# Two binary searches in an encoder step: VectorE's six tiles in one group, ScalarE on one tile throughout, and another order of masks and attention

## Chip, core and metric

The kernel runs on one core of a Trainium2 chip. The metric is the device time of one execution in microseconds. Engines go by the profile's names: PE is TensorE (PEld its weight loads), DVE is VectorE, ACT is ScalarE, POOL is GpSimd, and SP is SyncE, whose queue issues the transfers.

## What is computed

One layer of a streaming encoder on 1,024 prompt frames and 64 sample frames: a half-step feed-forward block, an input projection, a sparse attention branch and a convolution branch merged by gates, a second half-step block and a final normalization. The part that the change touches is the choice of keys:

```python
limit = (pos // CHUNK + 1) * CHUNK
admissible = key_pos[None, :] < limit[:, None]
s = jnp.einsum('bqhd,bsd->bqhs', qi, k_idx).astype(jnp.float32)
score = jnp.einsum('bqh,bqhs->bqs', wi.astype(jnp.float32), jax.nn.relu(s))
score = jnp.where(admissible[None], score, -jnp.inf)
_, sel = lax.top_k(score, top)             # top = min(256, L // 4)
...
p = jax.nn.softmax(logits, axis=-1)        # over the selected keys alone
o = jnp.einsum('bqcgn,bqncd->bqcgd', p, vg)
```

## The kernel before

**Search tiles.** `STILES` has seven tiles of query rows with their scores: tiles 0 to 5 have 128 rows and 384, 512, 640, 768, 896 and 1,024 keys; tile 6 is the sample, 64 rows and 192 keys. (The first 256 prompt rows need no search.) Attention numbers the same rows by `ATILES`: search tile n is attention tile n + 2, so that the widest is attention tile 7 and the sample is attention tile 8.

**The search.** The kernel finds, for each row, the value of its top-th score, bit by bit: first the 15 upper bits (`search(15, ...)`), then, after `low_half` has counted the rows above and taken out the lower halves, the 16 lower bits (`search(16, ...)`). A round of one bit has a count for every tile (how many scores are at least the candidate) and then a *settle* for a group of tiles: L909 (`low_`, the lower candidate), L911 (`flag`, count against target) and L913 (the next candidate). On VectorE a count is L902 with an accumulator; on ScalarE it is L899 (a Sign with an accumulated sum), settled by L920 and L921 for each tile by itself. `GROUPS` says who does what: in the 15-bit phase ScalarE has tile 5, VectorE the groups (4, 3, 1) and (2, 0, 6); in the 16-bit phase ScalarE has tiles 5 and 4, VectorE (3, 1) and (2, 0, 6). The two groups of VectorE take turns: one is settled between the counts of the other. `LEAD_X` lets ScalarE's rounds be written two ahead in the first phase. The targets `thr` and the low candidates `low_` lie in PSUM, the rest in SBUF.

**Masks.** After the search, L960 to L964 put the two halves together for each of the three groups, and then each tile has six operations on VectorE (L972 to L979: compare, equal, running count, need, and the mask `bias`). The code takes tiles 5, 4, 6, 3, 2, 1, 0. The masks read and write `Y` and `H16`, the scores and their upper halves, in the pool `low`.

**Gates.** While VectorE searches, PE computes 14 of 16 gate rows (`gates`, three chunks of 24 matmuls each), ACT evicts each chunk with a tanh (L1000), SP stores it, and POOL makes the low parts of the weights (L119) and sums a convolution with ACT (L674, L675).

**Attention.** When the pools `low` and `cvs` are closed, the attention pool `ap_` is opened in their place. A unit is one tile and two heads. `soft` computes logits (L1047, L1048, PE), adds the mask and takes the maximum (L1050, DVE), takes the exponential (L1060, ACT), and normalizes (L1062 DVE, L1064 one head on POOL, one on DVE); `turn` transposes two key blocks (L1074) and splits them (L152, L153); `values` multiplies. Two units are computed ahead (`AHEAD`). `TORD` is the order of the tiles, `FILL` how many steps of background work (the last two gate rows, the normalization and output of the convolution, then the merge) follow each turn. The query rows of the first tile are loaded early into the pool `ak`; those of the second go into `ap_`, the third again into `ak` (L683 the transfer, L686 and L687 the split).

**What sets the order.** The text of the kernel gives dependences and priorities (search and masks stand under `high_priority`); the framework's planner works out each engine's order of instructions from them and from its own estimate of times. Each engine then works through its list in that order.

Of the kernel before, what the change touches and what calls it, by code (L numbers as in the profile page):

```python
# [9 lines left out]
F32 = mybir.dt.float32  # L10
# [6 lines left out]
ALU = mybir.AluOpType  # L17
# [27 lines left out]
TORD = (7, 6, 8, 5, 4, 3, 2, 1, 0)  # L45
# [47 lines left out]
class Kern:  # L93
# [342 lines left out]
    def run(self):  # L436
        tc, nc, a = self.tc, self.nc, self.a
        PS = bass.MemoryType.PSUM
        with ExitStack() as top:
# [325 lines left out]
            thx = kp.tile([P, 2], F32, name="thx")  # L765
            lkx = kp.tile([P, 2], F32, name="lkx")

            COL = {n: c for c, n in enumerate((5, 4, 3, 1, 2, 0, 6))}
            GROUPS = {15: ((5,), (4, 3, 1), (2, 0, 6)), 16: ((5, 4), (3, 1), (2, 0, 6))}

            LEAD_X = {15: 2, 16: 0}

            def cols(g):
                return slice(COL[g[0]], COL[g[-1]] + 1)
# [6 lines left out]
            for n, (t0, rows, k0, L, top_) in enumerate(STILES):  # L781
                c = COL[n]
                nc.gpsimd.memset(ktop[:, c:c + 1], float(top_))
                nc.gpsimd.memset(lmk[:, c:c + 1], float(L - 2 * top_ + 1))
                if c < 2:
                    nc.gpsimd.memset(lkx[:, c:c + 1], -float(L + 1))
# [82 lines left out]
            def low_half(g):  # L869

                cg = cols(g)
                nc.vector.tensor_scalar(cand[:, cg], hib[:, cg], 1.0, None, op0=ALU.add)
                for n in g:
                    rows, y0, L = rows_of(n)
                    hh = H16[:rows, y0:y0 + L]
                    c1 = slice(COL[n], COL[n] + 1)
                    nc.vector.tensor_scalar(spare(n), hh, cand[:rows, c1], 0.0,
                                            op0=ALU.is_ge, op1=ALU.add, accum_out=cnt[:rows, c1])
                    lo16 = Y[:rows, y0:y0 + L].bitcast(U16).rearrange("p (n t) -> p n t", t=2)[:, :, 0]
                    nc.vector.scalar_tensor_tensor(hh.bitcast(U16), hh, hib[:rows, c1], lo16,  # L880
                                                   op0=ALU.is_equal, op1=ALU.mult)
                nc.vector.tensor_tensor(thr[:, cg], thr[:, cg], cnt[:, cg], op=ALU.subtract)
                nc.vector.memset(cand[:, cg], float(1 << 15) - 0.5)
                if g[0] in GROUPS[16][0]:
                    start_x(cg)

            def start_x(cg):
                nc.vector.scalar_tensor_tensor(thx[:, cg], thr[:, cg], 2.0, lkx[:, cg], op0=ALU.mult, op1=ALU.add)

            def search(bits, dt, res):  # L890

                XT, GA, GB = GROUPS[bits]

                def count(n, b):
# [3 lines left out]
                    if n in XT:  # L898
# [6 lines left out]
                def settle(t, b):  # L905

                    g = cols(t)
                    half = 0.5 * (1 << b)
                    nc.vector.tensor_scalar(low_[:, g], cand[:, g], -half, None, op0=ALU.add)  # L909
                    yield  # L910
                    nc.vector.tensor_tensor(flag[:, g], cnt[:, g], thr[:, g], op=ALU.is_ge)  # L911
                    yield
                    nc.vector.scalar_tensor_tensor((res if b == 0 else cand)[:, g], flag[:, g], 2 * half, low_[:, g],  # L913
                                                   op0=ALU.mult, op1=ALU.add)
                    yield

                def settle_x(n, b):

                    c = slice(COL[n], COL[n] + 1)
                    nc.scalar.activation(flag[:, c], cnt[:, c], AF.Sign, bias=thx[:, c])  # L920
                    nc.scalar.activation((res if b == 0 else cand)[:, c], flag[:, c], AF.Identity,  # L921
                                         bias=cand[:, c], scale=-0.5 * (1 << b))

                def xrounds():
                    for b in range(bits - 1, -1, -1):
                        for n in XT:
                            count(n, b)
                        for n in XT:
                            settle_x(n, b)
                        yield b  # L930
                    yield

                sb = iter(())
# [3 lines left out]
                for b in range(bits - 1, -1, -1):  # L937
                    if next(xs, 0) is None and bits == 15:
                        low_half(XT)
                    for n in GA:  # L940
                        count(n, b)
                        next(sb, None)
                    for _ in sb:
                        pass
                    sa = settle(GA, b)
                    for n in GB:
                        count(n, b)
                        next(sa)
                    sb = settle(GB, b)
                for _ in sb:  # L950
                    pass

            nc.vector.memset(cand, float(1 << 14) - 0.5)
            start_x(cols(GROUPS[15][0]))
            search(15, I16, hib)
            for g in ((4,), (3, 1), (2, 0, 6)):
                low_half(g)
            search(16, U16, lob)
            for g in map(cols, GROUPS[16]):
# [6 lines left out]
            for n in (5, 4, 6, 3, 2, 1, 0):  # L966
# [517 lines left out]
```

## Time and profile before

| | us |
|---|---|
| median of 3 runs | 2425.44 (2422.06 to 2425.85) |
| profiled execution | 2427.43 |
| its span (first to last instruction) | 2425.7 |
| PE busy in the span | 2311.7 (95%) |
| DVE busy in the span | 1769.9 (73%) |
| ACT / POOL busy in the span | 1207.6 (50%) / 1403.9 (58%) |
| mean granted PE clock | 0.982 of full |

Times in the trace count from the start of the span. The change lies between 1070 us, where the first count starts, and about 1550 us, where the attention ends. Before and after it there is only work that the change does not name. A timeline row has start, duration, engine, line and operation, and in brackets how long the engine stood idle before it and what released it.

### The profile page before, as it was taken

The page shows a single profiled execution, that of the slowest core. Times are in us where ns is not written, and L with a number is a line of the kernel's source. Part 1 is how long each engine was busy: PE and PEld are TensorE (multiplying, and loading weights), DVE is VectorE, ACT ScalarE, POOL GpSimd, SP SyncE. Part 2 cuts the span into 40 slices and gives each one's busy share as a digit, 9 for nine tenths or more (in the row PEclk, how much of TensorE's full clock was granted, in tenths as well). Part 3 has the DMA queues.
Part 4 walks back from the last instruction along what each step waited for, and adds up shares of the span by engine and source line. Part 5 has one row for each costly group of instructions (what it writes and reads, how often), then busy time and mean ns, then how long its engine had stood idle before and what let it go on. Part 6 is the DMA issues. An engine that isn't in the chain of part 4 may idle for free. (4 is left out here: it accounts for less than half of the span.)

```text
span 2425.7 us, 44597 instructions
## 1 busy us (share of the span) xinstructions
PE 2311.7 (95%) x16762; PEld 2279.0 (94%) x16762; DVE 1769.9 (73%) x4053; ACT 1207.6 (50%) x2363; POOL 1403.9 (58%) x866
## 2 busy tenths in 40 slices
PE   5999999999999999999878999799999999999998
PEld 5999999999999999999877889799999999999997
DVE  7666678666668287699998976758766777776666
ACT  5434345434336446868866555535433445343443
POOL 4555555555557686878733456447555555555554
PEclk9999999999999999999999999999999999999999
DMA  4232233223224434233222556563232322333333
GB/s 164 94 99 91 94 100 116 100 96 105 87 90 136 137 125 137 80 107 114 85 88 75 166 149 189 154 222 97 87 105 90 99 97 82 109 105 103 96 98 114
DMA packets 129977, 271.89 MB, mean 112 GB/s; under 512 B 17888, under 2 KB 77152, under 8 KB 129760
## 3 DMA queue, kind: packets, MB, share of 16 engines
q1 hardware_dynamic: 129760, 269.03, 34.8%
q8 instruction: 132, 2.16, 0.4%
q14 instruction: 85, 0.70, 0.1%
HBM read 230.29 MB, written 38.75 MB: 111 GB/s over the span
## 5 line engine op out<-in xcount | busy, mean ns | idle before, releaser
L119 POOL TENSOR_TENSOR wlo<-raw,whi 128x1024 fp32r<-128x1024 f32 (+1 forms) x187 | 437.0, 2341 | 380.5 <-ACT whi L118 375.9
L136 PE MATMUL ps<-x,wp 128*128 128x272 f32 x1760 | 508.2, 290 | 10.9 <-DVE spare L284 9.3
L138 PE MATMUL ps<-x,wp 128*128 128x272 f32 x1760 | 505.7, 290 | 0.8 <-DVE wp L153 0.6
L137 PE MATMUL ps<-x,wp 128*128 128x272 f32 x1760 | 506.4, 289 | 0.0
L136 PE MATMUL ps<-x,whi 128*128 128x272 f32 (+2 forms) x1544 | 484.6, 314 | 18.0 <-ACT sg L1000 8.3
L138 PE MATMUL ps<-x,wlo 128*128 128x272 f32 (+2 forms) x1544 | 483.0, 313 | 0.0
L137 PE MATMUL ps<-x,whi 128*128 128x272 f32 (+2 forms) x1334 | 413.1, 310 | 0.0
L136 PE MATMUL ps<-gh,whi 128*128 128x272 f32 x1408 | 400.2, 290 | 5.3 <-DVE spare L284 3.5
L137 PE MATMUL ps<-gl,whi 128*128 128x272 f32 x1408 | 405.2, 289 | 0.0
L138 PE MATMUL ps<-gh,wlo 128*128 128x272 f32 x1408 | 404.0, 289 | 0.0
L153 POOL TENSOR_TENSOR wlo<-raw,whi 128x1024 fp32r<-128x1024 f32 x88 | 218.9, 2489 | 266.9 <-ACT whi L152 263.5
L136 PEld LDWEIGHTS ps<-x,wp 128*128 128x128 f32 x1760 | 332.6, 189 | 11.7 <-ACT wp L152 11.6
L137 PEld LDWEIGHTS ps<-x,wp 128*128 128x128 f32 x1760 | 333.0, 189 | 0.0
L138 PEld LDWEIGHTS ps<-x,wp 128*128 128x128 f32 x1760 | 330.4, 189 | 2.3 <-DVE wp L153 2.0
L136 PEld LDWEIGHTS ps<-x,whi 128*128 128x128 f32 x1544 | 294.3, 191 | 21.0 <-ACT sg L1000 9.2
L153 POOL TENSOR_TENSOR wp<-s,wp 128x512 fp32r<-128x512 f32 x176 | 257.9, 1466 | 89.2 <-ACT wp L152 89.2
L118 ACT ACTIVATE whi<-raw 128x1024 fp32r<-128x1024 f32 (+1 forms) x187 | 190.6, 1020 | 222.8 <-PE ps L137 113.2
L424 DVE SCALAR_TENSOR_TENSOR h<-ps,h 128x272 f32<-128x272 f32 x384 | 164.7, 439 | 184.2 <-PE ps L138 183.7
L138 PEld LDWEIGHTS ps<-x,wlo 128*128 128x128 f32 x1544 | 294.1, 191 | 1.2
L675 POOL TENSOR_TENSOR ac<-ac,pd 128x559 f32<-128x559 f32 x180 | 259.7, 1443 | 57.8 <-ACT pd L674 26.8
L136 PEld LDWEIGHTS ps<-gh,whi 128*128 128x128 f32 x1408 | 263.5, 189 | 6.8 <-DVE spare L284 4.1
L138 PEld LDWEIGHTS ps<-gh,wlo 128*128 128x128 f32 x1408 | 266.2, 189 | 0.0
(230 smaller groups left out, 5009.6 us busy)
## 6 DMA issues: line engine op xcount, KB each, us to landing
raw<-wf SPq DMA_DIRECT2D x334, 512.0 KB, 3.4
raw<-wf SPq DMA_DIRECT2D x32, 384.0 KB, 3.1
d_g<-sg SPq DMA_DIRECT2D x32, 181.0 KB, 1.9
d_h<-h SPq DMA_DIRECT2D x2, 2176.0 KB, 10.7
y<-t SPq DMA_DIRECT2D x32, 136.0 KB, 1.9
raw<-d_q SPq DMA_DIRECT2D x32, 128.0 KB, 3.1
raw<-d_qi SPq DMA_DIRECT2D x24, 128.0 KB, 3.1
d_g<-sg SPq DMA_DIRECT2D x16, 182.0 KB, 2.9
```

Source lines behind the costliest of these rows:

```text
L118: nc.scalar.activation(hi[:, :n], raw[:, :n], AF.Copy)
L119: self.weng.tensor_tensor(lo[:, :n], raw[:, :n], hi[:, :n], op=ALU.subtract)
L136: t.matmul(out, wh, xh, start=first, stop=False)
L137: t.matmul(out, wh, xl, start=False, stop=False)
L138: t.matmul(out, wl, xh, start=False, stop=last)
L153: (eng or nc.vector).tensor_tensor(lo, x, hi, op=ALU.subtract)
L424: nc.vector.scalar_tensor_tensor(x, p, 0.5, x, op0=ALU.mult, op1=ALU.add)
L675: nc.gpsimd.tensor_tensor(ac, ac, pd, op=ALU.add)
```

## The change

The groups `GROUPS` go. ScalarE has tile 5 (`XT`) in both phases, with one column of targets. VectorE has the other six tiles (`VT`) in both phases, in the order 4, 6, 3, 2, 1, 0; they are counted one after the other and then settled by one L909, L911 and L913 over six columns, where there were two settles over two or three columns, woven into the counts. `low_half` is called twice (tile 5; the six) and not four times; the halves are put together for two groups and not for three. The masks are written in the order 6, 3, 4, 5, 2, 1, 0 (before: 5, 4, 6, 3, 2, 1, 0), and attention takes its tiles as 8, 5, 6, 7, 4, 3, 2, 1, 0 (before: 7, 6, 8, 5, 4, 3, 2, 1, 0).

```diff
@@ -42,7 +42,7 @@
 NOPEN = 3
 RAHEAD = 200
 PAHEAD = 60
-TORD = (7, 6, 8, 5, 4, 3, 2, 1, 0)
+TORD = (8, 5, 6, 7, 4, 3, 2, 1, 0)
 NLG, NPT = 3, 2
 GPRE = 14
 MS = lambda nc: set()
@@ -762,16 +762,13 @@
                 rows, y0, L = rows_of(n)
                 return bias[:rows, BOFF[n + 2]:BOFF[n + 2] + L]
 
-            thx = kp.tile([P, 2], F32, name="thx")
-            lkx = kp.tile([P, 2], F32, name="lkx")
-
-            COL = {n: c for c, n in enumerate((5, 4, 3, 1, 2, 0, 6))}
-            GROUPS = {15: ((5,), (4, 3, 1), (2, 0, 6)), 16: ((5, 4), (3, 1), (2, 0, 6))}
-
+            thx = kp.tile([P, 1], F32, name="thx")
+            lkx = kp.tile([P, 1], F32, name="lkx")
+
+            XT, VT = 5, (4, 6, 3, 2, 1, 0)
+            COL = {n: c for c, n in enumerate((XT, *VT))}
             LEAD_X = {15: 2, 16: 0}
-
-            def cols(g):
-                return slice(COL[g[0]], COL[g[-1]] + 1)
+            GX, GV = slice(0, 1), slice(1, NT)
             nc.gpsimd.memset(cnt, 0.0)
 
             def rows_of(n):
@@ -782,7 +779,7 @@
                 c = COL[n]
                 nc.gpsimd.memset(ktop[:, c:c + 1], float(top_))
                 nc.gpsimd.memset(lmk[:, c:c + 1], float(L - 2 * top_ + 1))
-                if c < 2:
+                if n == XT:
                     nc.gpsimd.memset(lkx[:, c:c + 1], -float(L + 1))
             def begin(ns):
 
@@ -866,11 +863,10 @@
             thr, low_ = sb_[:, 0:NT], sb_[:, 16:16 + NT]
             nc.vector.tensor_copy(thr, thr0)
 
-            def low_half(g):
-
-                cg = cols(g)
+            def low_half(ns, cg):
+
                 nc.vector.tensor_scalar(cand[:, cg], hib[:, cg], 1.0, None, op0=ALU.add)
-                for n in g:
+                for n in ns:
                     rows, y0, L = rows_of(n)
                     hh = H16[:rows, y0:y0 + L]
                     c1 = slice(COL[n], COL[n] + 1)
@@ -881,89 +877,62 @@
                                                    op0=ALU.is_equal, op1=ALU.mult)
                 nc.vector.tensor_tensor(thr[:, cg], thr[:, cg], cnt[:, cg], op=ALU.subtract)
                 nc.vector.memset(cand[:, cg], float(1 << 15) - 0.5)
-                if g[0] in GROUPS[16][0]:
-                    start_x(cg)
-
-            def start_x(cg):
-                nc.vector.scalar_tensor_tensor(thx[:, cg], thr[:, cg], 2.0, lkx[:, cg], op0=ALU.mult, op1=ALU.add)
+
+            def start_x():
+                nc.vector.scalar_tensor_tensor(thx, thr[:, GX], 2.0, lkx, op0=ALU.mult, op1=ALU.add)
 
             def search(bits, dt, res):
-
-                XT, GA, GB = GROUPS[bits]
 
                 def count(n, b):
                     rows, y0, L = rows_of(n)
                     c = COL[n]
                     v, c1 = H16[:rows, y0:y0 + L].bitcast(dt), cand[:rows, c:c + 1]
-                    if n in XT:
+                    if n == XT:
                         nc.scalar.activation(spare(n), v, AF.Sign, bias=c1, scale=-1.0,
                                              accum_out=cnt[:rows, c:c + 1])
                     else:
                         nc.vector.tensor_scalar(spare(n), v, c1, 0.0, op0=ALU.is_ge, op1=ALU.add,
                                                 accum_out=cnt[:rows, c:c + 1])
 
-                def settle(t, b):
-
-                    g = cols(t)
-                    half = 0.5 * (1 << b)
-                    nc.vector.tensor_scalar(low_[:, g], cand[:, g], -half, None, op0=ALU.add)
-                    yield
-                    nc.vector.tensor_tensor(flag[:, g], cnt[:, g], thr[:, g], op=ALU.is_ge)
-                    yield
-                    nc.vector.scalar_tensor_tensor((res if b == 0 else cand)[:, g], flag[:, g], 2 * half, low_[:, g],
-                                                   op0=ALU.mult, op1=ALU.add)
-                    yield
-
-                def settle_x(n, b):
-
-                    c = slice(COL[n], COL[n] + 1)
-                    nc.scalar.activation(flag[:, c], cnt[:, c], AF.Sign, bias=thx[:, c])
-                    nc.scalar.activation((res if b == 0 else cand)[:, c], flag[:, c], AF.Identity,
-                                         bias=cand[:, c], scale=-0.5 * (1 << b))
-
                 def xrounds():
+
                     for b in range(bits - 1, -1, -1):
-                        for n in XT:
-                            count(n, b)
-                        for n in XT:
-                            settle_x(n, b)
+                        count(XT, b)
+                        nc.scalar.activation(flag[:, GX], cnt[:, GX], AF.Sign, bias=thx)
+                        nc.scalar.activation((res if b == 0 else cand)[:, GX], flag[:, GX], AF.Identity,
+                                             bias=cand[:, GX], scale=-0.5 * (1 << b))
                         yield b
                     yield
 
-                sb = iter(())
                 xs = xrounds()
                 for _ in range(LEAD_X[bits]):
                     next(xs)
                 for b in range(bits - 1, -1, -1):
+                    half = 0.5 * (1 << b)
                     if next(xs, 0) is None and bits == 15:
-                        low_half(XT)
-                    for n in GA:
+                        low_half((XT,), GX)
+                        start_x()
+                    for i, n in enumerate(VT):
                         count(n, b)
-                        next(sb, None)
-                    for _ in sb:
-                        pass
-                    sa = settle(GA, b)
-                    for n in GB:
-                        count(n, b)
-                        next(sa)
-                    sb = settle(GB, b)
-                for _ in sb:
-                    pass
+                        if i == 0:
+                            nc.vector.tensor_scalar(low_[:, GV], cand[:, GV], -half, None, op0=ALU.add)
+                    nc.vector.tensor_tensor(flag[:, GV], cnt[:, GV], thr[:, GV], op=ALU.is_ge)
+                    nc.vector.scalar_tensor_tensor((res if b == 0 else cand)[:, GV], flag[:, GV], 2 * half, low_[:, GV],
+                                                   op0=ALU.mult, op1=ALU.add)
 
             nc.vector.memset(cand, float(1 << 14) - 0.5)
-            start_x(cols(GROUPS[15][0]))
+            start_x()
             search(15, I16, hib)
-            for g in ((4,), (3, 1), (2, 0, 6)):
-                low_half(g)
+            low_half(VT, GV)
             search(16, U16, lob)
-            for g in map(cols, GROUPS[16]):
+            for g in (GV, GX):
                 nc.vector.tensor_copy(mi[:, 0, g], hib[:, g])
                 nc.vector.tensor_copy(mi[:, 1, g], lob[:, g])
                 nc.vector.tensor_scalar(mi[:, 0, g], mi[:, 0, g], 16, None, op0=ALU.logical_shift_left)
                 nc.vector.tensor_tensor(mth[:, g].bitcast(I32), mi[:, 0, g], mi[:, 1, g], op=ALU.bitwise_or)
                 nc.vector.tensor_tensor(sth[:, g], mth[:, g], sgn[:, g], op=ALU.mult)
 
-            for n in (5, 4, 6, 3, 2, 1, 0):
+            for n in (6, 3, 4, XT, 2, 1, 0):
                 rows, y0, L = rows_of(n)
                 y = Y[:rows, y0:y0 + L]
                 b = bias[:rows, BOFF[n + 2]:BOFF[n + 2] + L]
```

## Rows read from the trace of the kernel before

**Rows 1.** The page's busy times: busy us, share of the span, instructions

```profile
PE 2311.7 (95%) x16762; PEld 2279.0 (94%) x16762; DVE 1769.9 (73%) x4053; ACT 1207.6 (50%) x2363; POOL 1403.9 (58%) x866
```

**Rows 2.** Busy us by stretch: from:to, length, engines (instructions), clock, DMA share, GB/s

```profile
1070.10:1163.50 93.40, 88.01 (x521) 87.42 (x520) 91.13 (x292) 72.79 (x138) 69.79 (x42) 0.98 0.39 115
...
1175.80:1242.30 66.50, 62.62 (x378) 62.33 (x376) 64.33 (x262) 66.49 (x149) 50.27 (x32) 0.99 0.31 103
1242.30:1277.00 34.70, 22.36 (x118) 21.49 (x118) 34.44 (x57) 7.53 (x17) 6.60 (x2) 0.80 0.15 52
...
1277.00:1292.00 15.00, 13.33 (x57) 11.15 (x58) 10.87 (x32) 8.85 (x13) 4.55 (x2) 0.83 0.34 94
...
1300.00:1347.00 47.00, 43.94 (x320) 39.83 (x319) 44.92 (x121) 32.08 (x66) 17.77 (x11) 1.00 0.27 75
```

**Rows 3.** Timeline of PE: matmuls that PE stood idle before

```profile
1157.80 0.43 PE L136 MATMUL ps<-x,whi 128*128 128x362 f32 x1 [3.78 <-ACT sg L1000]
...
1243.27 0.79 PE L1047 MATMUL lg<-kh,qt 128*128 128x512 f32 x1 [4.85 <-ACT sg L1000]
...
1277.80 0.79 PE L1047 MATMUL lg<-kh,qt 128*128 128x512 f32 x1 [12.16 <-DVE mb L1050]
```

**Rows 4.** Timeline of SP, DVE and ACT: second query tile, last mask operation

```profile
1114.06 1.45 SPq L683 DMA_DIRECT2D raw<-d_q  x3
...
1274.59 2.22 DVE L979 SCALAR_TENSOR_TENSOR bias<-bias,H 128x1024 bf16<-128x1024 bf16 x2
...
1276.96 1.06 ACT L686 ACTIVATE qt<-raw 128x1024 fp32r<-128x1024 f32 x1 [16.58 <-issue]
```

**Rows 5.** Timeline of DVE: pieces of one round of the 15-bit phase

```profile
1118.44 1.15 DVE L902 TENSOR_SCALAR_CACHE_REDUCE bias<-H,cand 128x896 bf16<-128x896 int16 x1
...
1119.51 0.16 DVE L909 TENSOR_SCALAR srch<-cand 128x3 f32<-128x3 f32 x1
1119.58 1.00 DVE L902 TENSOR_SCALAR_CACHE_REDUCE bias<-H,cand 128x768 bf16<-128x768 int16 x1
...
1121.17 0.15 DVE L911 TENSOR_TENSOR flag<-cnt,srch 128x3 f32<-128x3 f32 x1
...
1121.55 0.88 DVE L902 TENSOR_SCALAR_CACHE_REDUCE bias<-H,cand 128x640 bf16<-128x640 int16 x1
```

**Rows 6.** Groups by shape, 1060 to 1300 us: count, busy us, mean ns, idle before

```profile
L899 ACT ACTIVATE bias<-H,cand 128x896 bf16<-128x896 uint16 x16 | 16.7, 1045 | 4.5 <-DVE srch L882 4.4
...
L909 DVE TENSOR_SCALAR srch<-cand 128x3 f32<-128x3 f32 x46 | 7.3, 159 | 0.1
...
L909 DVE TENSOR_SCALAR srch<-cand 128x2 f32<-128x2 f32 x16 | 2.5, 157 | 0.0
```

**Rows 7.** Timeline of DVE and POOL: first mask operations and two held ones

```profile
1242.34 3.16 DVE L974 TENSOR_SCALAR H<-Y,mth 128x768 bf16<-128x768 f32 x2
...
1260.01 4.23 POOL L119 TENSOR_TENSOR wlo<-raw,whi 128x1024 fp32r<-128x1024 f32 x1 [14.80 <-ACT whi L118]
...
1261.88 2.38 DVE L961 CAST mi<-lob 128x2 int32<-128x2 f32 x1
...
1264.57 1.34 DVE L974 TENSOR_SCALAR H<-Y,mth 128x1024 bf16<-128x1024 f32 x2
```

**Rows 8.** Timeline of ACT and DVE: ScalarE's last first-phase settle, VectorE's use

```profile
1145.17 0.28 ACT L921 ACTIVATE hib<-flag,cand 128x1 f32<-128x1 f32 x1
...
1152.44 0.15 DVE L872 TENSOR_SCALAR cand<-hib 128x1 f32<-128x1 f32 x1
```

**Rows 9.** Instructions of L687: shortest, median, longest ns; first and last start

```profile
L687 DVE TENSOR_TENSOR qt<-raw,qt x16: 689/1223/2559, 926.2 to 1525.9; 64x1024 fp32r<-64x1024 f32 x14, 64x512 fp32r<-64x512 f32 x2
```

**Rows 10.** Timeline: first transposes of attention; a unit of the sample tile

```profile
1291.71 1.03 PE L1074 MATMUL pt<-ident,pr 128*128 128x128 f32 x8
...
1356.22 0.35 DVE L1050 CUSTOM_DVE_ANT_0 pr<-lg,bias 64x192 f32<-64x192 f32 x1
...
1361.24 0.30 DVE L1064 TENSOR_SCALAR pr<-pr,sm 64x192 f32<-64x192 f32 x1
```

## Prediction

> **What bounds the kernel now.** I read the page's busy times first: PE is busy for 95% of the span [rows 1], so in most of the kernel only PE's idle time can be won. The change lies in one stretch, so I then read the busy times by stretch [rows 2]. There the picture turns round. In the two phases of the search VectorE is busy for 91.13 of 93.40 us and 64.33 of 66.50 us, and in the masks for 34.44 of 34.70 us, where PE is busy for only 22.36 us. VectorE is thus the chain from the first count at 1070 us to the last mask at 1276.8 us; PE fills the time with gate rows. The third view is what PE stood idle for [rows 3]: 3.78 us and 4.85 us for ScalarE's evictions of gate chunks, which queue behind ScalarE's counts and waits, and 12.16 us for the masks.
>
> The next question is what opens the attention: the mask of its first tile, or the last mask of all. The rows on the second query tile tell [rows 4]. Its transfer was issued at 1114.06 us, yet ScalarE's split of it (L686) starts at 1276.96 us, after 16.58 us in which ScalarE did nothing and the trace names no wait. The last mask operation ends at 1274.59 + 2.22 = 1276.81 us, 0.15 us earlier. The split writes into the attention pool, which stands where the search's `Y` and `H16` stood. I read this as a wait for memory: the attention pool opens when the last mask has read its scores, whichever tile comes first. So PE's 12.16 us are the distance between "out of gates" and "last mask", and an idle time of PE that is saved earlier only makes this one longer.
>
> **The change, part by part.** All prices are VectorE's, from start to start of neighbouring instructions.
>
> *Settles.* L909 stands 46 + 16 = 62 times [rows 6], one for each settle; the change leaves 15 + 16 = 31. A settle takes 0.07 us for L909 (1119.51 to 1119.58) and 0.38 us for L911 and L913 (1121.17 to 1121.55) [rows 5], 0.45 us in all. 31 settles fewer: -14.0 us. The six columns cost no more than three to within what rows show of two against three (157 and 159 ns) [rows 6]. In one group each step uses the result of the step before. No row has six columns in a chain, but the 0.45 us already holds a flag that reads the count just ended and a candidate that reads that flag; I add nothing, and at most 0.2 us for each of 31 rounds (the gap of one dependent step, half of 0.38), +6.2 us.
>
> *Counts.* Tile 4 moves to VectorE for 16 rounds. Its count takes 1118.44 to 1119.51, 1.07 us [rows 5]: +17.1 us. ScalarE loses 16 counts of 1.045 us and their settles [rows 6], which takes nothing off the chain, because ScalarE's evictions matter to PE alone, and PE waits for the masks afterwards.
>
> *Small operations.* Two calls of `low_half` fewer and one group fewer in putting halves together are 12 small operations, at 0.07 to 0.19 us each (L909 alone, or half of the L911 and L913 pair) [rows 5]: -0.8 to -2.3 us, and I take -1.2.
>
> *The early query tile.* The first attention tile is now the sample, whose split L687 is half as wide: 0.69 against 1.22 us in the median, and 2.56 at the longest [rows 9]. -0.5 to -1.9 us during the search; I take -0.6, and the wide split comes back later, beside other work.
>
> *Holds by POOL.* L961 on two columns took 2.38 us while POOL's L119 ran from 1260.01 to 1264.24, and the first pair of L974 took 3.16 us against 1.34 us for a wider pair [rows 7]: two holds, 2.2 and 1.8 us, about 4 us in the masks. I leave them as they are; the bounds are none (-4) and twice as many (+4). The Trainium skill (SBUF — State Buffer, section "SBUF: two separate sides") says that VectorE's operations that use both ports, and GpSimd's, lock each other out for a whole instruction; the rows of L961 agree. [...]
>
> The last mask therefore moves by -14.0 + 17.1 - 1.2 - 0.6 = +1.3 us, to about 1278 us (from 1272 to 1288 with all bounds).
>
> *The order of masks.* By the memory reading it moves nothing at the start. *The order of attention* changes how it fills. Before, the widest tile comes first and the first transposes run at 1291.71 us [rows 10], 15 us after the opening. In those 15 us PE is idle for 1.67 us, and its mean clock of 0.83 means a third of the time at 1.2 GHz and not at 2.4, 2.5 us lost: 4.2 us together [rows 2]. A unit of the sample takes 5.3 us from its first masked logits (1356.22) to its last normalization (1361.24 + 0.30) [rows 10], amid other work, so its transposes can start some 9 us sooner. I take half of the 4.2 us, -2.1; the bounds are 0 (other work waits just the same) and -4.2. The background steps before the merge are as many in both orders (52 turns' worth by `FILL`), so nothing else is gained there; VectorE is busy 44.92 of the next 47 us [rows 2].
>
> Sum: +1.3 - 2.1 = -0.8 us on the profiled 2427.43 us (span 2425.7 us and 1.7 around it), which lies 2.0 us above the median. On the median: 2425.4 - 0.8 = **2424.6 us**.
>
> **The rivals.** *Faster by cleaner masks.* PE loses its earlier holes and runs some 9 us ahead (3.78 + 4.85) [rows 3], so POOL may have made the last weights before the masks begin; then both holds go and the fill gives all: +1.3 - 4 - 4.2 = -6.9, 2418.5 us. For it: only two L119 lie in the masks' stretch (POOL has 2 instructions there [rows 2]). Against: they are tied to PE's chunks, which may merely shift onto other masks. *Faster by an early opening.* If only some buffers of the attention pool lie on the search's memory, the sample's attention runs beneath the masks of the others and PE's 12.16 us shrink: up to +1.3 - 12.2 = -10.9, or, if VectorE stays the limit, +1.3 minus its 4.1 idle us after the opening [rows 2]; between 2414.5 and 2422.6 us, say 2418. Against: the 0.15 us [rows 4].
>
> *Faster by a fast count.* If VectorE counted these 16-bit scores four to a cycle, a count of tile 4 would take a quarter of 1.07 us and its 16 counts 4.3 us instead of 17.1: -0.8 - 12.8 = -13.6, 2411.8 us. Against it stands the row itself: 1.15 us for 896 columns [rows 5], nothing like a quarter of ScalarE's 1.045 us for the same tile [rows 6]. The Trainium skill (VectorE: DVE Perf Modes, section "The perf-mode tier table") lists `tensor_scalar` on 16-bit data in SBUF at four elements a cycle; the rows of this counting form do not agree.
>
> *Slower by the small tile first.* Four units of the sample come one behind another with two units of look-ahead; nothing wide is in the pipe to cover their chains. If one chain of 5.3 us [rows 10] lies open before the first wide unit flows, and the fill gives nothing back: +1.3 + 5.3 = +6.6, 2432 us. It decides from the point where the background steps (gates done before, normalization waiting for its transfer) are too few to feed PE for those 5 us. *Slower by ScalarE's lead.* ScalarE settles its last upper bit at 1145.45 us, VectorE uses it at 1152.44, 7.0 us later [rows 8]; 13 shorter rounds bring VectorE 5.9 us forward, which leaves 1.1 us. A miss by one round costs about 5 us: with no gain in the fill 2431.7 us. *It does not do what it says.* The text put tile 5's mask first, yet the 768-wide tile ran first [rows 7]: the planner may place the masks as before. By the memory reading that costs nothing; it is inside the forecast.
>
> **How the numbers follow.** About 0.2% (5 us) is what a measurement of this kernel can tell from no change. Forecast, within that: 0.41. Faster: cleaner masks 0.20, early opening 0.14, the fast count 0.01, together 0.35. Slower: small tile first 0.15, ScalarE's lead 0.09, together 0.24. The forecast's own range is 2420.5 to 2430.3 us. The range for 8 in 10 reaches to both sides: below to 2414.5, the early opening at its best; above to 2433, the small tile first with 1 us of holds.
>
> **What would show each step.** L909 31 times and two L902 of 896 columns where there was one, with rounds 0.45 us shorter in the first phase and 1.07 - 0.45 = 0.62 us longer in the second. ScalarE's hole for tile 4 gone. The last L979 at 1272 to 1288 us, ACT's L686 right behind it, and PE's wait for the masks longer than 12.16 us, some 20 us. The first transposes 5 to 9 us after the opening, not 15. The prediction is wrong if L1050 runs well before the last L979 (the memory reading falls), if the rounds of the second phase grow by over 0.9 us (the single chain has gaps), or if the attention from 1300 to 1550 us has grown or shrunk by more than 4 us, which I priced at nothing.

## The result: some 21 us slower

The changed kernel takes 2445.17 us in the median of six runs (2439.60 to 2445.99), the kernel before 2422.63 us (six runs, 2417.67 to 2425.85). The medians lie 22.5 us apart; the ratio is 1.0086 (some 21 us), with a 95% interval of 1.0076 to 1.0097. The forecast was 2424.6 us.

The profiled execution of the changed kernel has a span of 2443.0 us, 17.3 more than before. Its lines are renumbered: a count is L894 (before: L902), a settle L918 to L920 (L909 to L913), a mask ends with L948 (L979), logits are L1016 and L1017 (L1047, L1048), the masked maximum L1019 (L1050), the gates' eviction L969 (L1000).

The next rows are busy times by stretch, columns as in [rows 2]; first the kernel before, then the changed one. The first stretch of each starts with the counts (8.2 us behind the preparation of the 384-key tile) and ends with the last mask, which I call the opening; the second ends with the last eviction of attention (`oh`).

```profile
1070.13:1276.81 206.68, 182.36 (x1070) 180.29 (x1068) 202.17 (x642) 154.62 (x318) 133.41 (x80) 0.95 0.32 98
1276.81:1571.81 295.00, 268.20 (x1786) 249.85 (x1786) 231.60 (x607) 171.78 (x374) 143.89 (x77) 0.97 0.49 145
```

```profile
1070.65:1278.75 208.10, 171.99 (x1008) 170.33 (x1006) 204.93 (x569) 131.56 (x251) 132.66 (x79) 0.92 0.29 92
1278.75:1588.20 309.45, 278.80 (x1846) 259.42 (x1846) 238.00 (x608) 174.06 (x377) 144.64 (x78) 0.98 0.47 142
```

So the search and the masks grew by 1.4 us (forecast: 1.3), and the attention by 14.4. With 0.5 us of later start and 0.9 us behind the attention that is all of the 17.3 us. In the attention PE has 60 more matmuls and 10.6 us more of work, and stands idle for 3.8 us longer (309.45 - 278.80 against 295.00 - 268.20).

Which matmuls these are is seen in PE's groups after the opening, gates alone, the kernel before ahead of the changed one (columns: line, tile, count; busy, mean ns):

```profile
L138 PE MATMUL ps<-x,wlo 128*128 128x362 f32 x11 | 3.9, 357 | 0.0
L136 PE MATMUL ps<-x,whi 128*128 128x362 f32 x10 | 3.5, 349 | 0.0
L137 PE MATMUL ps<-x,whi 128*128 128x362 f32 x7 | 2.5, 350 | 0.0
L137 PE MATMUL ps<-u,whi 128*128 128x362 f32 x4 | 1.5, 374 | 0.0
```

```profile
L138 PE MATMUL ps<-x,wlo 128*128 128x362 f32 (+1 forms) x31 | 10.5, 339 | 0.0
L136 PE MATMUL ps<-x,whi 128*128 128x362 f32 (+1 forms) x30 | 10.3, 343 | 0.0
L137 PE MATMUL ps<-x,whi 128*128 128x362 f32 (+1 forms) x23 | 8.0, 346 | 0.0
L137 PE MATMUL ps<-u,whi 128*128 128x362 f32 (+1 forms) x8 | 2.6, 327 | 0.0
```

Of the 144 matmuls of the last two gate rows, 32 lay behind the opening before the change and 92 lie there now. One follows the other by 0.166 us (three in 0.50, next fence): 60 are 10.0 us. Where PE stood idle instead, its timeline shows:

```profile
1234.38 0.30 PE L1016 MATMUL lg<-kh,qt 128*64 128x192 f32 x1 [1.44 <-ACT sg L969]
...
1253.14 0.67 PE L136 MATMUL ps<-x,whi 128*128 128x364 f32 x1 [18.01 <-DVE lob L920]
...
1263.63 0.33 PE L136 MATMUL ps<-x,whi 128*128 128x362 f32 x1
...
1264.13 0.32 PE L136 MATMUL ps<-x,whi 128*128 128x362 f32 x1
1279.50 0.42 PE L1016 MATMUL lg<-kh,qt 128*64 128x192 f32 x1 [15.04 <-DVE mb L1019]
```

The first hole of 3.78 us in [rows 3] is gone, the second shrank from 4.85 to 1.44 us, and PE comes to the attention's first logits 8.9 us earlier. But then it waits 18.01 us for the end of the search, does 52 gate matmuls, and waits 15.04 us for the masks. Before, the search had ended when PE came to its first gate, as its last operation and that gate show:

```profile
1242.19 0.16 DVE L913 SCALAR_TENSOR_TENSOR lob<-flag,srch 128x3 f32<-128x3 f32 x1
...
1246.00 0.51 PE L136 MATMUL ps<-x,whi 128*128 128x364 f32 x1
```

So the gates began at once behind the first logits, and PE did 112 of them ahead of its 12.16 us. VectorE and ScalarE of the changed kernel show what stands around its two waits:

```profile
1252.93 0.15 DVE L920 SCALAR_TENSOR_TENSOR lob<-flag,srch 128x6 f32<-128x6 f32 x1
...
1274.73 4.02 DVE L948 SCALAR_TENSOR_TENSOR bias<-bias,H 64x192 bf16<-64x192 bf16 x6
...
1278.83 1.06 ACT L686 ACTIVATE qt<-raw 128x1024 fp32r<-128x1024 f32 x1 [18.36 <-DVE bias L948]
...
1282.10 0.54 ACT L969 ACTIVATE sg<-ps,hb 128x362 f32<-128x362 f32 x1
```

The search's small tile (`srch`) holds PSUM of a pool that the background gates take over, so they can't begin before its last operation, which now ends 10.7 us later (1253.08 against 1242.35 us in the trace of before); the masks end 1.9 us later. The stretch between, in which background gates can run, fell from 34.5 to 25.7 us. But it isn't full: PE stands idle in it for the 15.04 us, because its list, which the planner wrote, has 52 gate matmuls there and then logits that wait for the masks. ScalarE's list has the second query tile's split there, which waits for the last mask [rows 4, as before], and the next gate eviction stands behind it. So it is the order of the lists that puts the other 92 behind the opening.

### The profile page after: what moved, and what is told of

Read it like the earlier page. It is cut to its first block, busy times and chain, and to the rows that moved or that the text cites. A ratio compares the mean times of both kernels' runs of the same rounds, so it can differ in the third digit from the quotient of the medians.

```text
span 2443.0 us, 44444 instructions
## 1 busy us (share of the span) xinstructions
PE 2311.2 (95%) x16762; PEld 2277.2 (93%) x16762; DVE 1778.9 (73%) x3980; ACT 1187.5 (49%) x2299; POOL 1406.0 (58%) x865
## 5 line engine op out<-in xcount | busy, mean ns | idle before, releaser
L119 POOL TENSOR_TENSOR wlo<-raw,whi 128x1024 fp32r<-128x1024 f32 (+1 forms) x187 | 435.7, 2334 | 365.3 <-ACT whi L118 356.8
## 6 DMA issues: line engine op xcount, KB each, us to landing
d_h<-h SPq DMA_DIRECT2D x2, 2176.0 KB, 10.4
```

The source lines that it names most:

```text
L119: self.weng.tensor_tensor(lo[:, :n], raw[:, :n], hi[:, :n], op=ALU.subtract)
```

## The experiments

All kernels in one table. "Search, masks" is from the start of the preparation row of the 384-key tile to the end of the last mask, "attention" from there to its last eviction; "gates behind" are gate matmuls behind the opening. These are from one profiled execution each; ratios are against the kernel before, measured beside each run, with their 95% intervals.

| | search, masks | gates behind | attention | rest | median us | ratio |
|---|---|---|---|---|---|---|
| before | 214.9 | 32 | 295.0 | 853.9 | 2422.63 | |
| changed | 216.3 | 92 | 309.4 | 854.8 | 2445.17 | 1.0086 (1.0076, 1.0097) |
| search_only | 217.7 | 93 | 312.8 | 853.7 | 2446.48 | 1.0095 (1.0078, 1.0112) |
| orders_only | 212.9 | 31 | 302.7 | 854.1 | 2431.46 | 1.0027 (1.0018, 1.0037) |
| one_x | 232.0 | 38 | 305.5 | 853.3 | 2453.39 | 1.0110 (1.0092, 1.0128) |
| one_group | 204.5 | 34 | 307.7 | 854.3 | 2427.74 | 1.0007 (0.9997, 1.0017) |
| one_group_new | 203.3 | 31 | 298.9 | 854.6 | 2419.49 | 0.9976 (0.9966, 0.9985) |
| after_g16 | 218.7 | 0 | 298.7 | 853.4 | 2435.13 | 1.0047 (1.0032, 1.0062) |
| after_g15 | 216.5 | 44 | 300.4 | 855.6 | 2434.82 | 1.0035 (1.0022, 1.0048) |
| search_g15 | 217.8 | 47 | 312.0 | 848.6 | 2438.83 | 1.0057 (1.0041, 1.0074) |
| before_g16 | 216.8 | 0 | 300.2 | 864.0 | 2443.69 | 1.0078 (1.0061, 1.0095) |
| after_fill1 | 216.4 | 92 | 305.0 | 867.6 | 2450.31 | 1.0118 (1.0100, 1.0136) |
| after_psf | 216.6 | 92 | 312.1 | 854.2 | 2443.51 | 1.0088 (1.0069, 1.0108) |
| after_bank2 | 221.7 | 96 | 310.1 | 855.0 | 2449.68 | 1.0102 (1.0086, 1.0117) |

**The change in halves: search_only and orders_only.** The first is the changed kernel with this edit back; the second is the kernel before with both lines new.

```diff
-TORD = (8, 5, 6, 7, 4, 3, 2, 1, 0)
+TORD = (7, 6, 8, 5, 4, 3, 2, 1, 0)
-            for n in (6, 3, 4, XT, 2, 1, 0):
+            for n in (XT, 4, 6, 3, 2, 1, 0):
```

> The new search alone; masks and attention in the order of before. Theory A (the gates): the search ends 10 us later, so that the bank of the search's small tile comes free later, and the planner's list has 51 gate matmuls between the first logits and the logits that wait for the masks, where before it has 112; some 60 matmuls of 0.166 us come behind the opening. The time is then 2440 to 2446 us, with the wait for the end of the search (18 us after the changed kernel's first logits) in it. Theory B (the sample first): the loss comes from the order of attention, and the search alone moves the last mask by 2 us: 2422 to 2427 us.

> The old search; the new orders of masks and attention. Theory A: 113 gate matmuls stand ahead of the opening, as before; the time is that of before or some us under it, 2416 to 2426 us. Theory B: VectorE stands idle in the ramp (6.2 us before its first wide logits in the changed kernel) and loses 7 us or more of attention work: 2430 to 2440 us.

The search alone brings the whole loss (2446.48 us) with the same wait (17.27 us for the search's end) and 93 gates behind. That is theory A as far as it says that the loss comes with the search and the gates (the time is 0.5 us above its range); that the later end of the search is what puts them behind is not shown, and the next runs speak against it. The orders alone cost some 6.5 us, all of it in the attention (+7.7 us, with 31 gates behind), so theory B has a part where the search is the old one. In the changed kernel the order brings no loss on top: its median is 1.3 us under search_only's, and the intervals of the two ratios overlap.

**The search in halves: one_x and one_group.** one_x changes one tuple of the kernel before:

```diff
-16: ((5, 4), (3, 1), (2, 0, 6))}
+16: ((5,), (4, 3, 1), (2, 0, 6))}
```

one_group is the changed kernel in which ScalarE counts and settles tiles 5 and 4 in the second phase, and the old orders stand:

```diff
-            XT, VT = 5, (4, 6, 3, 2, 1, 0)
+            XS = {15: (5,), 16: (5, 4)}
+            VS = {15: (4, 6, 3, 2, 1, 0), 16: (6, 3, 2, 1, 0)}
...
+                XT, VT = XS[bits], VS[bits]
```

> The kernel before (its two groups on VectorE, its orders) with the one change that ScalarE counts only tile 5 in the second phase, tile 4 going to VectorE's group (4, 3, 1). Theory of the sum: 16 counts of 1.07 us come onto VectorE's chain, rounds of the second phase grow from 4.15 to 5.22 us, the last mask moves by +17 us to 1294 us, and with 106 gate matmuls ahead of the opening (before 112) the time grows by 15 to 19 us, to 2438 to 2444 us. Rival, that only gates moved behind the opening cost anything: 6 matmuls, 1 us, 2424 to 2427 us.

> The other half of the search change: VectorE settles its tiles as one group (six in the first phase, five in the second), while ScalarE keeps tiles 5 and 4 in the second phase; masks and attention in the order of before. By the sum with its settle term as predicted, 31 settles of 0.45 us fall away and the last mask comes 14 us earlier; with the gaps that the changed kernel's rounds show (4.905 us and not 4.78) 10 us earlier, at 1267 us. The planner's list has 110 gate matmuls ahead of the opening. Theory A (nothing is moved behind the opening): PE's wait for the masks (12.16 us) shrinks to 2 to 4 us and the time falls by 8 to 12 us, to 2412 to 2417 us. Rival (VectorE's single chain is no gain, or PE is the bound at the opening): 2421 to 2426 us.

The two terms of the sum are measured by themselves here. Tile 4's counts: the opening comes 17.1 us later, which is the forecast term to the tenth. Settles as one group: 10.4 us earlier, where 14.0 (and 1.2 for small operations) were forecast. The sum of the halves is +6.7 us, but both together moved it by 2.8 (search_only): the halves don't simply add up. PE's holes of one_x, then of one_group, ahead of the opening:

```profile
1266.47 0.67 PE L136 MATMUL ps<-x,whi 128*128 128x364 f32 x1 [31.72 <-DVE lob L913]
...
1292.73 0.80 PE L1047 MATMUL lg<-kh,qt 128*128 128x512 f32 x1 [6.58 <-DVE mb L1050]
```

```profile
1240.79 0.80 PE L1024 MATMUL lg<-kh,qt 128*128 128x512 f32 x1 [5.34 <-ACT sg L977]
...
1267.51 0.80 PE L1024 MATMUL lg<-kh,qt 128*128 128x512 f32 x1 [5.17 <-DVE mb L1027]
```

Where the search ends later, the gates wait for it (31.72 us); where it ends earlier, they don't. Neither half puts gates behind the opening: 38 and 34, before 32. In one_x the search ends at 1266.41 us, later than in the changed kernel, the gates wait for it longer, and the stretch up to the opening is narrower (25.2 us); still 106 gate matmuls lie in it. So neither that wait nor the narrower stretch moves gates behind the opening by itself. Only both halves together do (93 in search_only); why the planner's list is another one then is not shown. Both kernels take some 10 us more than even the upper end of what the theory had expected, though, because the attention takes 305.5 and 307.7 us with nearly as many gates behind as before. In one_group PE needs 276.27 us for 1,788 matmuls at a mean granted clock of 0.95, before 268.20 us for 1,786 at 0.97. That is 8.1 of its 12.7 us; the rest is PE's idle time. Why the clock dips there and not before isn't settled.

**one_group with the sample first.** `TORD` and nothing else.

> As one_group, with the sample first in the order of attention. The list has 113 gate matmuls ahead of the opening. The sample-first order alone cost 6.5 us with the old search: by that 2419 to 2424 us; if the order costs nothing where the opening comes early, 2412 to 2417 us.

Faster than the kernel before, by 0.24%. The time lies in the first range, but not for its reason: against one_group the sample first gains 8.8 us of attention here, and it lost 7.7 with the old search. The order of attention has no price of its own.

**More gate rows ahead: after_g15, after_g16, search_g15, before_g16.** `GPRE` is 15 or 16 in place of 14, nothing else.

> The changed kernel with all 16 gate rows ahead of the attention, so that no gate matmul needs the search's bank. Theory A: 92 gate matmuls that stood behind the opening (15 us) come ahead of it into PE's idle time, the 18 us wait goes, and the time falls by 8 to 15 us, to 2430 to 2437 us. Theory B: the sample's units lose what covers their chains, and the time stays at 2445 us or rises.

> The changed kernel with 15 gate rows ahead of the attention in place of 14: 28 gate matmuls in the list ahead of the logits that wait for the masks, 44 behind, so 48 fewer behind the opening than in the changed kernel. Theory A (0.166 us for each): 8 us faster, 2435 to 2439 us. Rival (the gates behind the opening are cover that the sample's ramp needs): 2443 to 2449 us.

> The new search with the old order of masks and attention and 15 gate rows ahead; 25 gate matmuls in the list ahead of the waiting logits, 47 behind (the run with the sample first and 15 rows: 44, 2434.8 us). By the count of gates alone 46 fewer than in search_only: 8 us under its 2446.5, 2437 to 2440 us. If the widest tile first fits better at few gates, as in the kernel before: 2428 to 2434 us.

> The kernel before with all 16 gate rows ahead of the attention. Theory A: 32 gate matmuls (5.3 us) come ahead of the opening, and the time falls by up to 5 us, to 2417 to 2423 us. Theory B says nothing of it beyond that the ramp loses cover: 2422 to 2428 us.

With 48 fewer gate matmuls behind the opening the changed kernel's attention falls by 9.1 us (8.0 by the count), the opening standing still. That undoes the loss by way of the gates, but the agreement is partly luck: PE's busy time falls by only 2.2 us, at a mean granted clock of 0.96 where the changed kernel has 0.98, and its idle time by 6.9 us. With 92 fewer the attention falls by 10.7 and not by 15.3: in the first 40 us behind the opening PE stands idle for 8.6 us, in the changed kernel for 3.2, so the last gates are also cover for the ramp. Before_g16 missed: with no gates behind, attention and merge lose 5.2 and 10.1 us, and PE stands idle in the attention for 5.5 us longer. Gates need nothing of VectorE; without them the first background steps are those of the normalization, which do, and PE's list has them right behind the first logits. So "as many gates ahead as possible" is no rule. Search_g15 falls as expected in its time, but not in its place: its attention stays at 312 us, because PE's busy time falls by 7.8 us (46 gates by the count: 7.6) and its idle time grows by 7.0. 5.1 us of its gain lie behind the attention (848.6 us), 2.1 ahead of the first count. Why PE waits longer there I can't explain.

**The wait or the number of gates: after_psf, after_bank2, after_bank, after_sbuf.** Four ways to take the search's PSUM out of the gates' way, each in the changed kernel. After_psf opens the pool `psf` ahead of `lg`. After_bank2 and after_bank give `srch` a pool of one bank, taken from `ps4` or from `lgi`. After_sbuf puts it into SBUF:

```diff
-            sb_ = lgi.tile([P, 512], F32, name="srch", tag="lgi")
+            sb_ = kp.tile([P, 32], F32, name="srch")
```

> The changed kernel with the background's PSUM pool opened ahead of the logits' pool, so that it takes banks that the search doesn't use. The planner's order of PE's instructions stays the same (52 gate matmuls, then the logits that wait for the masks), but the first of the 52 waits for nothing of the search. Theory A1 (the bank wait itself costs): PE's 18 us wait goes, and the time falls by 8 to 12 us, to 2433 to 2437 us. Theory A2 (only the order counts): the 52 come at 1236 us, PE then waits 30 us or more in one piece for the masks, and the time stays at 2443 to 2447 us.

> The changed kernel with a bank of its own for the search's targets, taken from the four of the gates' pool. No background gate then waits for the end of the search, but the planner's list has only 24 of the 144 background gate matmuls ahead of the logits that wait for the masks (changed kernel: 52). If the wait itself costs: 2433 to 2440 us. If the number behind the opening decides (120 against 92, 0.166 us each): 4 to 5 us slower than the changed kernel, 2447 to 2452 us, with PE idle for 35 us or more in one piece ahead of the opening.

> The changed kernel with a PSUM bank of its own for the search's targets and low candidates (the logits of the search keep three banks of four); VectorE's operations stay as they are. The bank is taken again only by attention's last pool, so that the background gates don't wait for the search's end. The planner's list then has all 144 background gate matmuls ahead of the logits that wait for the masks (changed kernel: 52). Theory A (bank and list): PE's 18 us wait for the end of the search is gone, the opening stays at 216 to 218 us after the first counts, no gate matmul lies behind it, and the attention shrinks from 309 to about 300 us, as in the run with 16 rows ahead: 2432 to 2437 us. Rival (the wait costs nothing, because PE waits for the masks anyway, as the prediction had it): 2443 to 2447 us.

> The changed kernel with the search's targets and low candidates in SBUF in place of PSUM, so that no bank hangs on the end of the search. Theory A1 (the bank wait itself costs): the 18 us wait goes, PE does its gates from 1235 us on, and the time falls by 8 to 12 us, to 2433 to 2437 us. Theory A2 (the planner's list decides): the list now has only 28 gate matmuls ahead of the next logits, 24 fewer than the changed kernel, PE stands idle for longer behind them, and the time rises by 0 to 4 us, to 2445 to 2449 us.

The first logits' hole in after_psf, and the one hole of after_bank2, which begins 29.5 us ahead of its opening:

```profile
1251.48 0.39 PE L1016 MATMUL lg<-kh,qt 128*64 128x192 f32 x1 [20.40 <-issue]
```

```profile
1281.69 0.67 PE L136 MATMUL ps<-x,whi 128*128 128x362 f32 x1 [31.20 <-ACT sg L970]
```

After_psf told nothing: the wait moved onto the first logits. After_bank2 separates the two, though its list left 96 gates behind and not the 120 expected. No gate waits for the search's end, yet all 96 stay behind the opening, because PE now waits 31.20 us for ScalarE's eviction, behind the split that waits for the masks; and the attention takes 310.1 us, as in the changed kernel. (Of the 2.2 us between the two profiled executions 1.2 lie ahead of the opening.) So nothing was gained by taking away the wait for the bank alone; in these runs of the changed kernel the attention goes with how many gates are left behind. After_bank (2465.47 us, 1.0161) and after_sbuf (2473.62 us, 1.0198) are slower for other reasons: with a logits bank less the preparation row comes 24.7 us later and the counts 31.4, and in SBUF the settles are held (last section). Their attention goes with the gates too: after_bank has none behind and 299.6 us, after_sbuf 116 and 313.5 us, which is 4.1 us more than the changed kernel for 24 more gates (4.0 by the count). The same bank in the kernel before and in one_group_new misses in the same way, with the preparation row 22.6 and 24.6 us later: 2467.99 us (1.0173) and 2451.14 us (1.0105).

> The kernel before with the bank of its own: 144 gate matmuls in the list ahead of the logits that wait for the masks (before: 112). By 0.166 us for each gate matmul that comes forward: 5 us faster, 2418 to 2422 us. If the widest tile's ramp needs gates as cover (the run with 16 rows ahead rose by 19 us, 10 of them at the merge): 2428 to 2440 us.

> The fastest so far (one group on VectorE, ScalarE with two tiles in the second phase, sample first) with the bank of its own. 144 gate matmuls lie ahead of the opening, 31 more than without. If each is worth 0.166 us, PE's 4.5 us wait for the masks fills up and the time falls by 3 to 5 us, to 2414 to 2417 us. If gates in the ramp are the cover that its chains need, it rises by 0 to 5 us, to 2419 to 2425 us.

**The hole in the ramp: after_fill1, ogn_fill1, ogn_g15.** In the changed kernel VectorE stands idle for 6.18 us up to 1300.14 us, behind the first piece of the wide logits and ahead of the next, while PE does 48 gate matmuls in a row:

```profile
1300.14 0.56 DVE L1019 CUSTOM_DVE_ANT_0 pr<-lg,bias 128x384 f32<-128x384 f32 x1 [6.18 <-PE lg L1017]
```

After_fill1 is the changed kernel with the edit below, ogn_fill1 is one_group_new with it, and ogn_g15 is one_group_new with `GPRE` 15:

```diff
-FILL = {7: 1, 6: 1, 8: 2, 5: 1, 4: 1, 3: 2, 2: 2, 1: 2, 0: 2}
+FILL = {7: 1, 6: 1, 8: 1, 5: 1, 4: 1, 3: 2, 2: 2, 1: 2, 0: 2}
```

> The changed kernel with one background step after each turn of the sample in place of two (FILL[8] 1). 52 gate matmuls stay ahead of the opening; those behind it now lie scattered between the wide tile's logits and not 48 in a row ahead of them. If VectorE's hole of 6.2 us behind the sample is part of the loss: 4 to 7 us faster, 2438 to 2441 us. If PE's 92 matmuls are the loss wherever they stand behind the opening: 2443 to 2447 us.

> One group on VectorE, ScalarE with tiles 5 and 4 in the second phase, sample first (2419.5 us), with FILL[8] 1. The list's beginning is the same; four background steps come later. By the hole: 2416 to 2420 us, no change, since its gates (31 behind the opening) were never in a row there. By a merge that starts later: 2420 to 2424 us.

> The same kernel of 2419.5 us with 15 gate rows ahead: 44 gate matmuls ahead of the logits that wait for the masks, some 28 behind. Nearly as many behind as with 14 rows (31), so by the count of gates no change: 2417 to 2421 us; if PE's wait for the masks is filled better, down to 2414 us.

The longest wait of VectorE for the wide logits in that place and, later, PE at the merge, in after_fill1:

```profile
1296.04 0.56 DVE L1019 CUSTOM_DVE_ANT_0 pr<-lg,bias 128x384 f32<-128x384 f32 x1 [1.17 <-PE lg L1017]
```

```profile
1598.62 0.64 PE L136 MATMUL ps<-xh,whi 128*128 128x362 f32 x1 [13.13 <-DVE ga L1179]
```

The hole falls to 1.17 us and the attention by 4.4 us, to 305.0: about what the hole was worth. But the background is then four steps behind, the merge waits 13.13 us, where the changed kernel waits 4.83 us, and the time rises. With one_group_new neither edit makes a difference: 2418.52 us (0.9981; 0.9971 to 0.9991) and 2418.55 us (0.9976; 0.9963 to 0.9989). These three, with VectorE in one group and ScalarE with two tiles in the second phase, beat both kernels.

## Why the prediction was wrong

- *The last mask, +1.3 us:* +1.4, which is luck: the terms were off and made up for each other. The counts were right: 17.1 us. The saving by settles was priced too high. A round is 4.91 us (next fence, 1229.64 to 1234.55), not 4.77: 0.31 us shorter than before and not 0.45, and in the second phase 0.75 longer and not 0.62. From the last accumulator to the next count, flag and candidate take 0.51 us where 0.38 were priced; that is the bound for dependent steps (up to 0.2 us for each round), which I had named and left at nothing. 31 rounds of 0.13 are 4.0 us. What made up for it: the early split gave more than its 0.6 us (0.88 us against 2.56), and POOL has no instruction at all between 1253.10 and 1278.75 us, so the holds of the masks [rows 7], some 4 us, are gone, which I had as a rival. One of about their length came into the search instead: L929 on six columns took 2.39 us at 1157.88, while POOL's L119 ran.

```profile
1229.64 1.15 DVE L894 TENSOR_SCALAR_CACHE_REDUCE bias<-H,cand 128x896 bf16<-128x896 uint16 x1
...
1234.04 0.08 DVE L894 DVE_READ_ACCUMULATOR bias<-H,cand 128x1 f32 x1
1234.15 0.16 DVE L919 TENSOR_TENSOR flag<-cnt,srch 128x6 f32<-128x6 f32 x1
1234.35 0.16 DVE L920 SCALAR_TENSOR_TENSOR cand<-flag,srch 128x6 f32<-128x6 f32 x1
1234.55 1.15 DVE L894 TENSOR_SCALAR_CACHE_REDUCE bias<-H,cand 128x896 bf16<-128x896 uint16 x1
```

- *Memory opens the attention:* borne out. L686 starts 0.08 us behind the last mask, which the trace now names as what released it (L948; last fence of the section on the result), though it reads nothing of it; L1019 follows.
- *The step that failed:* "PE waits for the masks afterwards" and "an idle time of PE that is saved earlier only makes this one longer", with the background steps counted as "52 turns' worth by `FILL`". I took PE's 12.16 us for the whole of its slack ahead of the opening, never asked what it did in the 20 us before them, and so put the work that could move behind the opening at nothing. It did 112 matmuls of the background there. In the changed kernel it does 52; the other 60, 10.0 us, lie in the attention, though PE stands idle for 15.04 us ahead of the opening. The counts by turns say how many steps follow each turn, not how many of them are done by then. A row could have told that there was work to lose: PE's wait in [rows 3] ends at 1243.27, and gate matmuls begin at 1246.00 us, while the last settle ended at 1242.35. That the planner would leave them behind could not be read there.
- *PE's wait for the masks, "some 20 us":* 15.04 us, and 18.01 us ahead of it, for the search. This sign was there; I had read it as harmless.
- *The ramp, -2.1 us:* the transposes do start 5.4 us behind the opening (1284.17 us; forecast 5 to 9), but VectorE is busy for only 9.08 of the 21.25 us up to 1300.00, PE for 20.50, with 48 gates in a row. After_fill1 shows that this is part of the loss: without that row the attention was 4.4 us shorter.
- *The rivals:* "slower by the small tile first" named the place and not the mechanism; its chains were covered, by gates that stood in the way (PE's 20.50 of 21.25 us). "ScalarE's lead" did not come: VectorE stood idle for 3.2 us from the first count to the opening, before for 4.5 us. The sign that I set for a wrong prediction, the attention changing by more than 4 us, is the one that came.
- *What stays open:* why the planner's lists have 52 gate matmuls ahead of the opening where both halves of the search change, and 106 and 110 where one does (one_x, one_group). The gates explain 10.0 of the attention's 14.4 us, the rest is mostly PE's idle time (3.8 us) and partly the hole in the ramp; the two overlap. Besides, with 31 to 47 gates behind, attention took from 295.0 us (before) to 312.0 us (search_g15). The kernel before has the shortest of all these runs; what makes it fit so well was not found.

## What to carry to other kernels

A wait that ends a stretch doesn't make all slack ahead of it free: ask of each engine what it did in the stretch, and what it costs if that work is done later. Room for the work is not enough: an edit can change the order that a planner writes, so that an engine waits with the work behind it in its list. Count in the new trace what lies on either side of the wait. And measure two halves of a change apart: here one (settles in one group) was good for 10 us of the search, the other (tile 4's counts) cost 17, and only both together moved the gates.

## What the hardware showed

Small operations of six columns are held by POOL when both inputs lie in SBUF. L919 takes 159 ns in the mean with the targets in PSUM (first fence, the changed kernel) and 659 ns with them in SBUF (after_sbuf); 31 of them make 15.5 us. The first two fences are groups of VectorE, the third is after_sbuf's timeline.

```profile
L919 DVE TENSOR_TENSOR flag<-cnt,srch 128x6 f32<-128x6 f32 x31 | 4.9, 159 | 0.9
```

```profile
L919 DVE TENSOR_TENSOR flag<-cnt,srch 128x6 f32<-128x6 f32 x31 | 20.4, 659 | 0.9
```

```profile
1135.91 4.36 POOL L675 TENSOR_TENSOR ac<-ac,pd 128x559 f32<-128x559 f32 x3 [0.22 <-ACT pd L674]
...
1137.54 1.26 DVE L919 TENSOR_TENSOR flag<-cnt,srch 128x6 f32<-128x6 f32 x1
```

The Trainium skill (SBUF — State Buffer, section "SBUF: two separate sides") gives the rule: a VectorE operation with two SBUF inputs and a GpSimd operation that reads SBUF exclude each other for a whole instruction. These rows agree. With the targets in PSUM none of these was held: the longest L919 of the changed kernel took 164 ns.
